# Block sums of an FFN written one tile ahead of their low parts, PSUM copies and weight sums in another order

## The chip, the cores and the metric

The kernel runs on one core of a Trainium2 chip. The metric is device microseconds of one execution; a time stands for the median of several runs. TensorE (PE) multiplies 128x128 blocks into PSUM, VectorE (DVE) and ScalarE (ACT) do the elementwise work, SyncE (SP) and GpSimd (POOL) issue the transfers.

## The reference

One decoder block on 1024 tokens of width 1024, all in float32. The change touches only the entry of its last part, the feed-forward network:

```python
h2 = rmsnorm(x, norm2_g[l]) * (1.0 + sc2) + sh2
fg, fu = jnp.split(h2 @ w_ffn_in[l], 2, axis=-1)
x = x + gt2 * ((jax.nn.silu(fg) * fu) @ w_ffn_out[l])
```

`h2` is 1024x1024, `w_ffn_in` 1024x5632 (2816 columns for `fg`, 2816 for `fu`). Ahead of it stand the attention branch, the convolution branch and the output projection, behind it the product with `w_ffn_out` and a last norm.

## The kernel before

Activations lie transposed: tile `x1[m]` (m = 0 to 7) holds 128 of the 1024 features for all tokens, the first half of the tokens in its columns up to 512 and the second half behind them. For a result near float32 each operand is kept as a high part, rounded to the type fp32r, and a low part (the operand less its high part); `mm3` issues three matmuls for one product of blocks: high by high, low by high, high by low. ScalarE writes the high part (`split_hi`, or an activation with a bias), VectorE subtracts to get the low part, so each split goes VectorE, ScalarE, VectorE.

The product `h2 @ w_ffn_in` is done in a form of seven block products instead of eight (class `Pair`, its table `PRODUCTS`). The activations are cut in four blocks A11, A12, A21, A22 (features by tokens), 256 columns of the weights in B11 to B22. Sums of blocks are formed: on the activation side S1, S2, S3, S4 (four tiles each, in place of `x1`'s columns), on the weight side T1, T2, T3, T4 (names `tt`, two halves of one tile `t` per pair). Product `p` of a pair is 12 matmuls of 512 columns into bank X, Z or Y (`fx`, `fz`, `fy`). Banks X and Z go on accumulating after a part of them has been copied out: `keep` copies a bank into a `kept` tile on ScalarE, `out` adds it and makes the hidden tile `g`. A product that accumulates into a bank waits until the copies out of it are done.

Pairs come in order 0 to 21. Even pairs belong to `fg`, odd ones to `fu`. The first two pairs are done together, since the activation sums are formed while they run: this is the code written out at the end of the function's FFN entry (from `both(6, 7)` on). There the order on each of TensorE, VectorE and ScalarE is the order of the code (`in_order(True, (T, V, A))`), and an engine works strictly down its list. It goes: products 0 and 5 (on A11 and A12), S1 and product 1, S2 and product 2, S4 and product 3, S3 and product 4, A22 and product 6. `staged(f, g)` runs two functions over the four tiles of a block: in the kernel before, `g(j-1)` (the low part of a tile) is written ahead of `f(j)` (scaling and sum of the next one). `evacuations(p)` calls `keep` or `out` for both pairs; the numbers of `both(...)` count weight blocks: 6 and 7 are T2, 8 and 9 B22, 10 and 11 T3, 12 and 13 T4 of the pairs 0 and 1, 14 and 15 B11 and T1 of pair 2, 16 its T2. From product 14 on (pair 2) the loop prepares up to two weight blocks ahead of each product, at most six ahead.

Of the kernel before, what the change touches and what calls it, by code (L numbers as in the profile page):

```python
# [30 lines left out]
HB = 512  # L31
# [62 lines left out]
def tile_hybrid_block(ctx: ExitStack, tc: tile.TileContext, xT, vecs, cvec, lamv, relb, bsel, bmask, jrev,  # L94
# [39 lines left out]
    def slot(name, dt=F32):  # L134
        return sp.tile([P, S], dt, tag="s4", name=name)

    def t2(name, dt=F32):
        return tp.tile([P, HB], dt, tag="t2", name=name)
# [13 lines left out]
    def split_hi(dst, src, scale=1.0):  # L152
        return A.activation(dst, src, AF.Copy, scale=scale)
# [11 lines left out]
    class Weights:  # L165
# [13 lines left out]
        def high(self):  # L179
            self.hi = wp.tile([P, D], F32R, tag="whi", name=f"wh_{self.name}")  # L180
            split_hi(self.hi[:, :self.n], self.raw[:, :self.n])

        def low(self):
            self.lo = wp.tile([P, D], F32R, tag="wlo", name=f"wl_{self.name}")
            V.tensor_tensor(out=self.lo[:, :self.n], in0=self.raw[:, :self.n], in1=self.hi.bitcast(F32)[:, :self.n],
                            op=ALU.subtract)
# [178 lines left out]
    with tc.tile_pool(name="psS", bufs=2, space=bass.MemoryType.PSUM) as psS, \  # L365
# [54 lines left out]
        with tc.tile_pool(name="st", bufs=2) as st:  # L420
# [61 lines left out]
            for k in range(KD):  # L482
# [3 lines left out]
                if k in KS:  # L486
                    j = KS.index(k)
# [408 lines left out]
    with tc.tile_pool(name="ps2", bufs=6, space=bass.MemoryType.PSUM) as ps2, ExitStack() as fxs:  # L896
# [69 lines left out]
        stages = dict(zip(CN, (cn.means, cn.center, squares, cn.scales, cn.finish)))  # L966
# [185 lines left out]
        class Pair:  # L1152
# [33 lines left out]
            def prepare(self, p):  # L1186
                self.low(self.high(p))

            def high(self, p):
                name = self.PRODUCTS[p][1]  # L1190
                src = self.source(name)
                w = self.w[name] = weight_block()
                split_hi(w[:, :HB], src)
                return w, src
# [70 lines left out]
        def weight_block():  # L1265
            n = nblock[0] % NWB
            nblock[0] += 1
            if n < NWB - 4:
                return fx[0].tile([P, D], F32R, tag="wb", name="wb", bufs=NWB - 4)
            return wp.tile([P, D], F32R, tag="whi" if n % 2 else "wlo", name="wbp")  # L1270
# [5 lines left out]
        def both(*ns):  # L1276

            parts = [(order[n][0], order[n][0].high(order[n][1])) for n in ns]
            for g, part in parts:
                g.low(part)  # L1280

        def staged(*stages):

            for i in range(KH + len(stages) - 1):
                for k, f in reversed(list(enumerate(stages))):
                    if 0 <= i - k < KH:
                        f(i - k)

        def new_block(name):
            acts[name] = [None] * KH  # L1290

        sums1 = {}

        def scale1(j):

            for m in (j, KH + j):
                norms[1].scale(m)
            acts["S1"][j] = slot(f"S1_{j}", F32R)
            t = sums1[j] = t2("s1")
            V.tensor_tensor(out=t, in0=x1[j][:, HB:], in1=x1[KH + j][:, HB:], op=ALU.add)  # L1300
            A.activation(acts["S1"][j][:, :HB], t, AF.Identity, bias=bsum[:, j:j + 1])
            for m in (j, KH + j):
                norms[1].shift(m)
# [14 lines left out]
        def sums(j):  # L1318

            a11, a21, a22 = x1[j][:, :HB], x1[j][:, HB:], x1[KH + j][:, HB:]  # L1320
            V.tensor_tensor(out=a21, in0=a11, in1=a21, op=ALU.subtract)
            V.tensor_tensor(out=a11, in0=a22, in1=a21, op=ALU.subtract)
            high("S2", j, a11)

        def sum4(j):
            a12 = x1[KH + j][:, :HB]
            V.tensor_tensor(out=a12, in0=a12, in1=x1[j][:, :HB], op=ALU.subtract)
            high("S4", j, a12)

        def blocks(name, get):  # L1330
            new_block(name)
            staged(lambda j: high(name, j, get(j)), lambda j: low(name, j, get(j)))
# [8 lines left out]
        two = pairs[:2]  # L1341
        V.tensor_tensor(out=bsum, in0=cols[:, 3 * KD:3 * KD + KH], in1=cols[:, 3 * KD + KH:4 * KD], op=ALU.add)

        def products(p):
            for k in range(KH):
                for g in two:
                    g.product(p, (k,))

        def evacuations(p):
            for g in two:  # L1350
                g.evacuate(p)

        both(6, 7)
        two[0].product(0)
        norms[1].stat()
        both(8, 9)
        two[1].product(0)
        new_block("S1")
        for g in two:
            g.product(5)  # L1360
        staged(scale1, low1)
        evacuations(0)
        products(1)
        evacuations(5)
        new_block("S2")
        staged(sums, lambda j: low("S2", j, x1[j][:, :HB]))
        evacuations(1)
        products(2)
        new_block("S4")
        staged(sum4, lambda j: low("S4", j, x1[KH + j][:, :HB]))  # L1370
        evacuations(2)
        products(3)
        both(10, 11)
        both(12, 13)
        pairs[2].load()
        pairs[3].load()
        blocks("S3", lambda j: x1[j][:, HB:])
        evacuations(3)
        for g in two:
            g.product(4)  # L1380
        blocks("A22", lambda j: x1[KH + j][:, HB:])
        both(14, 15)
        evacuations(4)
        for g in two:
            g.product(6)
        both(16)
        evacuations(6)
        nprep = 17

        late = {}  # L1390
# [40 lines left out]
        for gi, grp in enumerate(groups):  # L1431
# [17 lines left out]
            else:  # L1449
# [36 lines left out]
                for i, hs in enumerate(parts):  # L1486
# [3 lines left out]
                    for m in range(KD):  # L1490
# [4 lines left out]
                        t = x1[m][:, hs]  # L1495
# [83 lines left out]
```

## Time and profile before

| | |
|---|---|
| median of 3 runs | 1428.28 us (1426.91 to 1430.82) |
| the profiled execution | 1425.09 us, of which its span is 1423.3 us |
| TensorE busy | 1365.6 us (96% of the span), 6178 matmuls |
| VectorE busy | 982.9 us (69%) |
| ScalarE busy | 599.3 us (42%) |
| the first two FFN pairs | from 719 to 787 us of the span |

Busy time of TensorE counts pipelined matmuls, which overlap by some 0.16 us each, so 96% is not full speed. In the timeline a row is an instruction or a run of like ones on one engine with its start, its duration and, in brackets, how long the engine was idle before it and which engine's result ended that.

### The profile page before, as it was taken

The page shows a single profiled execution, that of the slowest core. Times are in us where ns is not written, and L with a number is a line of the kernel's source. Part 1 is how long each engine was busy: PE and PEld are TensorE (multiplying, and loading weights), DVE is VectorE, ACT ScalarE, POOL GpSimd, SP SyncE. Part 2 cuts the span into 40 slices and gives each one's busy share as a digit, 9 for nine tenths or more (in the row PEclk, how much of TensorE's full clock was granted, in tenths as well). Part 3 has the DMA queues.
Part 4 walks back from the last instruction along what each step waited for, and adds up shares of the span by engine and source line. Part 5 has one row for each costly group of instructions (what it writes and reads, how often), then busy time and mean ns, then how long its engine had stood idle before and what let it go on. Part 6 is the DMA issues. An engine that isn't in the chain of part 4 may idle for free.

```text
span 1423.3 us, 16124 instructions
## 1 busy us (share of the span) xinstructions
PE 1365.6 (96%) x6178; PEld 1114.0 (78%) x6178; DVE 982.9 (69%) x1588; ACT 599.3 (42%) x974; POOL 72.0 (5%) x84
## 2 busy tenths in 40 slices
PE   6799999999999999999977999999999999999996
PEld 4578888777788887888755888888888888888886
DVE  6947688899989897897868556666555555434345
ACT  4437676676611115632664433333333332202145
POOL 3400000000000000000100000000000000000004
PEclk8999999999999999999998999999999999999998
DMA  7511000100112123349501233332222335413203
GB/s 275 194 29 45 30 31 30 35 26 30 45 45 59 45 80 97 105 160 345 191 29 59 89 119 118 119 113 80 79 85 89 111 126 177 144 45 104 78 16 119
DMA packets 44271, 135.11 MB, mean 95 GB/s; under 512 B 4857, under 2 KB 7841, under 8 KB 44194
## 3 DMA queue, kind: packets, MB, share of 16 engines
q1 hardware_dynamic: 39458, 118.88, 25.1%
q0 software_dynamic: 4160, 14.68, 3.0%
q8 instruction: 48, 0.79, 0.2%
q10 hardware_dynamic: 576, 0.52, 0.1%
q14 instruction: 29, 0.24, 0.1%
HBM read 115.19 MB, written 18.88 MB: 94 GB/s over the span
## 4 chain that ended last, share of the span: by engine, by line
PE 79%; DVE 10%; ACT 6%; DMA 3%; issue 1%; POOL 1%; SPq 0%; DVEq 0%; ACTq 0%; POOLq 0%
PE fx L107 16%; PE fo L119 16%; PE proj L107 8%; PE fz L107 8%; PE gc L107 6%; PE ga L107 5%; PE fy L107 4%; PE oc L119 3%; PE oa L107 3%; PE wo L119 2%; PE sc L107 2%; DVE adac L119 2%; PE av L107 2%; DMA ada<-in_w_ada 1%; DMA wr_wo<-in_w_out 1%
## 5 line engine op out<-in xcount | busy, mean ns | idle before, releaser
L119 DVE SCALAR_TENSOR_TENSOR x1r<-fo,cols,x1r 128x512 f32<-128x512 f32 (+1 forms) x72 | 49.3, 689 | 119.8 <-PE fo L119 119.5
L119 PE MATMUL fo<-gl,wh_fo 128*128 128x512 f32 x288 | 112.2, 389 | 0.0
L119 PE MATMUL fo<-gh,wl_fo 128*128 128x512 f32 x288 | 112.1, 389 | 0.0
L119 PE MATMUL fo<-gh,wh_fo 128*128 128x512 f32 x288 | 111.9, 389 | 0.0
L107 DVE SCALAR_TENSOR_TENSOR cacc<-u,vec,cacc 128x1022 f32<-128x1022 f32 (+28 forms) x87 | 110.2, 1267 | 2.2
L107 PE MATMUL proj<-hhi,wh_in 128*128 128x512 f32 x239 | 98.3, 411 | 1.8 <-DVE kl L119 1.8
L107 PE MATMUL proj<-hhi,wl_in 128*128 128x512 f32 x240 | 94.0, 392 | 0.0
L107 PE MATMUL proj<-hlo,wh_in 128*128 128x512 f32 x240 | 93.7, 390 | 0.0
L107 PE MATMUL fz<-S,wb 128*128 128x512 f32 x312 | 76.5, 391 | 5.1 <-ACT S L107 4.3
L107 PE MATMUL fx<-S,wb 128*128 128x512 f32 x312 | 77.4, 398 | 3.6 <-ACT S L107 3.5
L107 PE MATMUL fx<-A,wb 128*128 128x512 f32 x335 | 79.2, 391 | 1.7 <-DVE g L107 1.7
L119 ACT ACTIVATE wh_fo<-wr_fo 128x768 fp32r<-128x768 f32 x24 | 20.3, 846 | 136.0 <-PE fo L119 130.5
L107 PEld LDWEIGHTS fx<-A,wb 128*128 128x128 f32 x335 | 62.8, 188 | 15.5 <-issue 2.5
L107 PEld LDWEIGHTS fx<-S,wb 128*128 128x128 f32 x312 | 60.0, 193 | 17.1 <-ACT S L107 4.0
L107 PEld LDWEIGHTS fz<-S,wb 128*128 128x128 f32 x312 | 58.2, 188 | 19.3 <-ACT S L107 5.6
L107 DVE TENSOR_TENSOR wb<-tt,wb 128x512 fp32r<-128x512 f32 x52 | 35.8, 692 | 45.4 <-ACT wb L107 45.1
L119 PEld LDWEIGHTS fo<-gl,wh_fo 128*128 128x128 f32 x288 | 54.1, 188 | 11.6 <-DVE gl L119 0.4
L119 PEld LDWEIGHTS fo<-gh,wh_fo 128*128 128x128 f32 x288 | 54.1, 188 | 11.3
L119 PEld LDWEIGHTS fo<-gh,wl_fo 128*128 128x128 f32 x288 | 54.1, 188 | 11.1
L107 PE MATMUL fx<-S,wbp 128*128 128x512 f32 x216 | 55.7, 408 | 5.3 <-ACT S L107 5.1
L107 ACT ACTIVATE wb<-tt 128x512 fp32r<-128x512 f32 x52 | 32.7, 629 | 61.7 <-DVE tt L107 61.5
L119 ACT ACTIVATE e<-sc,mn 128x512 f32<-128x512 f32 (+7 forms) x64 | 47.2, 740 | 26.9 <-DVE mn L119 25.9
(333 smaller groups left out, 3409.7 us busy)
## 6 DMA issues: line engine op xcount, KB each, us to landing
ada<-in_w_ada SPq DMA_DIRECT2D x32, 512.0 KB, 4.3
rawu<-in_w_fi SPq DMA_DIRECT2D x22, 512.0 KB, 3.5
rawg<-in_w_fi SPq DMA_DIRECT2D x22, 512.0 KB, 4.4
g_d<-g POOLq DMA_DIRECT2D x20, 512.0 KB, 4.2
gl<-g_d SPq DMA_DIRECT2D x20, 512.0 KB, 6.2
wr_fo<-in_w_fo SPq DMA_DIRECT2D x24, 384.0 KB, 3.1
adac<-in_w_ada SPq DMA_DIRECT2D x16, 512.0 KB, 4.3
wr_wo<-in_w_out SPq DMA_DIRECT2D x16, 512.0 KB, 5.2
```

The lines of the kernel that those rows point to most:

```text
L107: self.last = f(*args, **kw)
L119: self.last = self.chain(f, *args, **kw) if self.chain else f(*args, **kw)
```

## The change

In seven places the order of the instructions is changed; what is computed stays the same.

- `staged` no longer reverses its stages: `f(j)`, the scaling and sum of the next tile, is written ahead of `g(j-1)`, the low part of the tile before. All five blocks that use it are affected (S1, S2, S4, S3, A22).
- The S1 sums go into the free upper half of the pairs' `t` tiles instead of tiles of the pool `t2`.
- `both(8, 9)` moves ahead of the second norm's statistic.
- `evacuations(0)` moves ahead of S1, `evacuations(5)` behind S2.
- T3 and T4 of both pairs are computed one after the other, and `high` finds them there. The loads of pairs 2 and 3 are issued right behind them.
- `both(12, 13)` moves behind product 4, `both(14, 15)` behind product 6.
- `prepare(16)` moves behind `evacuations(6)`.

```diff
-                src = self.source(name)
+                src = self.b[name] if name in self.b else self.source(name)
...
-                for k, f in reversed(list(enumerate(stages))):
+                for k, f in enumerate(stages):
...
-            t = sums1[j] = t2("s1")
+            t = sums1[j] = two[j % 2].t[:, HB:]
...
-        both(6, 7)
+        both(6, 7, 8, 9)
         two[0].product(0)
         norms[1].stat()
-        both(8, 9)
         two[1].product(0)
+        evacuations(0)
         new_block("S1")
         for g in two:
             g.product(5)
         staged(scale1, low1)
-        evacuations(0)
         products(1)
-        evacuations(5)
         new_block("S2")
         staged(sums, lambda j: low("S2", j, x1[j][:, :HB]))
+        evacuations(5)
         evacuations(1)
         products(2)
         new_block("S4")
         staged(sum4, lambda j: low("S4", j, x1[KH + j][:, :HB]))
         evacuations(2)
         products(3)
-        both(10, 11)
-        both(12, 13)
+        for t in ("T3", "T4"):
+            for g in two:
+                g.source(t)
         pairs[2].load()
         pairs[3].load()
+        both(10, 11)
         blocks("S3", lambda j: x1[j][:, HB:])
         evacuations(3)
         for g in two:
             g.product(4)
+        both(12, 13)
         blocks("A22", lambda j: x1[KH + j][:, HB:])
-        both(14, 15)
         evacuations(4)
         for g in two:
             g.product(6)
-        both(16)
+        both(14, 15)
         evacuations(6)
+        prepare(16)
```

VectorE at S1, tiles 0 and 1 (`x_0_...` and `x_4_...` are `x1[0]` and `x1[4]`, `s_...` and now `tt` the sum, `S_0_...` the tile whose low part is written):

```order
 L107 SCALAR_TENSOR_TENSOR x_0_4949<-x_0_4949,cols,rstd 128x512
 L107 SCALAR_TENSOR_TENSOR x_4_5112<-x_4_5112,cols,rstd 128x512
-L107 TENSOR_TENSOR s_5749<-x_0_4949,x_4_5112 128x512
-L107 SCALAR_TENSOR_TENSOR S_0_5748<-s_5749,small,S_0_5748 128x512
+L107 TENSOR_TENSOR tt<-x_0_4949,x_4_5112 128x512
 L107 SCALAR_TENSOR_TENSOR x_1_4992<-x_1_4992,cols,rstd 128x512
 L107 SCALAR_TENSOR_TENSOR x_5_5150<-x_5_5150,cols,rstd 128x512
-L107 TENSOR_TENSOR s_5758<-x_1_4992,x_5_5150 128x512
-L107 SCALAR_TENSOR_TENSOR S_1_5757<-s_5758,small,S_1_5757 128x512
+L107 TENSOR_TENSOR tt<-x_1_4992,x_5_5150 128x512
+L107 SCALAR_TENSOR_TENSOR S_0_5752<-tt,small,S_0_5752 128x512
```

The low part of tile 0 now stands behind the sum of tile 1; the others follow in the same way.

VectorE from the last tile of S2 to the first of S4 (`g_...`, `kepta`: the three instructions of `evacuations(5)`, which stood ahead of S2 before):

```order
+L107 TENSOR_TENSOR S_2_5819<-x_2_5030,S_2_5819 128x512
+L107 TENSOR_TENSOR S_3_5824<-x_3_5068,S_3_5824 128x512
+L107 TENSOR_TENSOR g_5828<-fy,kepta 128x512
+L107 TENSOR_TENSOR kepta<-fy,kepta 128x512
+L107 TENSOR_TENSOR g_5828<-kepta,g_5828 128x512
 L107 TENSOR_TENSOR x_4_5112<-x_4_5112,x_0_4949 128x512
-L107 TENSOR_TENSOR S_0_5866<-x_4_5112,S_0_5866 128x512
 L107 TENSOR_TENSOR x_5_5150<-x_5_5150,x_1_4992 128x512
+L107 TENSOR_TENSOR S_0_5862<-x_4_5112,S_0_5862 128x512
```

S4 begins behind the copies out of bank Y, and its low parts too are one tile late.

ScalarE from the second norm's statistic to S1 (`rstd` is the norm's factor by Ln and Exp, `wbp` the high parts of weight blocks 8 and 9, `kepta` the copies of `evacuations(0)`):

```order
+L107 ACTIVATE wbp<-rawg 128x512
+L119 ACTIVATE sq<-x_7_5282 128x512
+L107 ACTIVATE wbp<-rawu 128x512
 L107 ACT_TABLE_LOAD
-L119 ACTIVATE sq<-x_7_5282 128x512
-L107 ACTIVATE rstd<-st_5694,small 128x512
+L107 ACTIVATE rstd<-st_5700,small 128x512
 L107 ACT_TABLE_LOAD
 L107 ACTIVATE rstd<-rstd 128x512
-L107 ACTIVATE wbp<-rawg 128x512
-L107 ACTIVATE wbp<-rawu 128x512
-L107 ACTIVATE S_0_5748<-s_5749,small 128x512
+L107 ACTIVATE kepta<-fx 128x512 x2
+L107 ACTIVATE S_0_5752<-tt,small 128x512
```

The two high parts stand ahead of Ln and Exp, and the copies out of bank X between Exp and the first high part of S1.

## Rows read from the trace of the kernel before

**Rows 1.** Busy time by stretch: us, then each engine's busy time, TensorE's granted clock, DMA
```profile
719.00:787.00 68.00, 51.42 (x177) 34.89 (x176) 47.68 (x74) 35.38 (x56) 1.08 (x2) 0.90 0.11 43
787.00:1400.00 613.00, 613.00 (x2759) 509.33 (x2758) 326.68 (x483) 204.59 (x322) 16.69 (x24) 1.00 0.29 99
```

**Rows 2.** Timeline of TensorE: start, us, what, and the idle time before it
```profile
731.78 1.56 PE L107 MATMUL fz<-S,wb 128*128 128x512 f32 x6
...
748.90 7.69 PE L107 MATMUL fx<-S,wbp 128*128 128x512 f32 x18 [4.63 <-ACT S L107]
...
770.72 8.28 PE L107 MATMUL fx<-S,wb 128*128 128x512 f32 x24 [3.54 <-ACT S L107]
780.66 8.42 PE L107 MATMUL fx<-A,wb 128*128 128x512 f32 x36 [1.66 <-DVE g L107]
```

**Rows 3.** Timeline of VectorE from the second norm to the last wait
```profile
726.97 0.69 DVE L107 TENSOR_TENSOR wbp<-rawg,wbp 128x512 fp32r<-128x512 f32 x1 [5.15 <-ACT wbp L107]
...
728.18 1.41 DVE L107 SCALAR_TENSOR_TENSOR x<-x,cols,rstd 128x512 f32<-128x512 f32 x2
729.62 0.69 DVE L107 TENSOR_TENSOR s<-x,x 128x512 f32<-128x512 f32 x1
731.11 0.75 DVE L107 SCALAR_TENSOR_TENSOR S<-s,small,S 128x512 fp32r<-128x512 f32 x1 [0.80 <-ACT S L107]
...
742.03 0.75 DVE L107 SCALAR_TENSOR_TENSOR S<-s,small,S 128x512 fp32r<-128x512 f32 x1 [0.79 <-ACT S L107]
743.74 0.69 DVE L107 TENSOR_TENSOR g<-fy,kepta 128x512 f32<-128x512 f32 x1 [0.96 <-ACT kepta L107]
...
746.16 0.69 DVE L107 TENSOR_TENSOR g<-kepta,g 128x512 f32<-128x512 f32 x1 [1.14 <-ACT g L107]
746.77 0.68 DVE L107 TENSOR_TENSOR x<-x 128x512 f32<-128x512 f32 x1
747.49 0.69 DVE L107 TENSOR_TENSOR x<-x,x 128x512 f32<-128x512 f32 x1
748.88 0.69 DVE L107 TENSOR_TENSOR S<-x,S 128x512 fp32r<-128x512 f32 x1 [0.69 <-ACT S L107]
...
757.63 0.69 DVE L107 TENSOR_TENSOR x<-x,x 128x512 f32<-128x512 f32 x1
...
765.60 0.69 DVE L107 TENSOR_TENSOR tt<-rawg 128x512 f32<-128x512 f32 x1
...
770.79 2.49 DVE L107 TENSOR_TENSOR S<-x,S 128x512 fp32r<-128x512 f32 x4
...
779.83 0.68 DVE L107 TENSOR_TENSOR g<-fx,keptc 128x512 f32<-128x512 f32 x1
```

**Rows 4.** Timeline of ScalarE in the same stretch
```profile
723.78 0.69 ACT L107 ACTIVATE rstd<-st,small 128x512 f32<-128x512 f32 x1 [1.22 <-PE st L107]
...
725.78 0.63 ACT L107 ACTIVATE rstd<-rstd 128x512 f32<-128x512 f32 x1
...
743.13 1.06 ACT L107 ACTIVATE kepta<-fx 128x512 f32<-128x512 f32 x2
744.21 1.28 ACT L107 ACT_TABLE_LOAD   x1
...
770.05 2.18 ACT L107 ACTIVATE S<-x 128x512 fp32r<-128x512 f32 x4
```

**Rows 5.** Busy time by stretch where the granted clock was low, columns as above
```profile
748.00:757.00 9.00, 7.69 (x18) 4.82 (x18) 6.13 (x10) 2.53 (x5) 0.00 (x0) 0.62 0.00 0
...
767.00:777.00 10.00, 6.45 (x17) 4.67 (x17) 9.65 (x16) 6.57 (x12) 0.00 (x0) 0.66 0.56 210
...
1414.00:1416.00 2.00, 1.15 (x2) 0.43 (x2) 0.00 (x0) 1.26 (x3) 1.19 (x2) 0.52 0.50 175
```

**Rows 6.** Timeline of TensorE at the kernel's end
```profile
1412.44 2.72 PE L119 MATMUL stf<-sq,ones 128*128 128x256 f32 x6 [2.49 <-DVE sq L119]
```

**Rows 7.** DMA issues of the page: out<-in, KB each, us to landing
```profile
rawg<-in_w_fi SPq DMA_DIRECT2D x22, 512.0 KB, 4.4
```

## The prediction

> **What bounds the kernel now.** I read busy time by stretch first. From 787 to 1400 us TensorE is busy all the time at the full clock; from 719 to 787 it is busy 51.4 of 68.0 us and its clock averages 0.90 [rows 1]. The change touches only this stretch; what it gains there moves everything behind it, which runs at TensorE's pace and has no wait to take the gain back. So the question is when product 6 of the first two pairs can start, 780.66 us before.
>
> Then the timeline of TensorE: every long wait in the stretch is for S, A or g, results of ScalarE or VectorE [rows 2]. VectorE and ScalarE are themselves busy 47.7 and 35.4 us only [rows 1], and the timeline of VectorE shows why: it waits 0.69 to 0.80 us for ScalarE's high part before each low part, tile after tile [rows 3], while ScalarE waits for VectorE's next sum. The two take turns. The chain from the norm to product 6 is VectorE's list with these waits in it; I work the new list through in the same way.
>
> **Durations.** On VectorE a tensor_tensor starts 0.60 us after the one ahead where nothing holds it (four in 2.49 us, 0.69 each), and 0.72 after one that it depends on (746.77 to 747.49). A scalar_tensor_tensor frees VectorE after 0.67 (two in 1.41). From the end of a sum to the start of its low part, through ScalarE, 0.70 us pass (747.49 + 0.69 to 748.88), 0.80 in S1 (730.31 to 731.11) [rows 3]. I take these for the new order too. The bounds are 0.60 and 0.69 per instruction beside a busy ScalarE; the nearest row is the one where both engines run four S instructions at once, 770.05 and 770.79, and neither is slowed [rows 3, 4]: I take 0.60.
>
> **The change step by step**, from the first scaling (728.18) on:
>
> 1. *Blocks 8 and 9 ahead of the norm.* Exp ends at 725.78 + 0.63 = 726.41 [rows 4]. Scaling now starts 1.77 us later, since two high parts and two low parts stand between [rows 3]. They move to where VectorE idles 5.15 us and ScalarE 1.22 us before Ln [rows 3, 4]; two copies of 0.53 fit in 1.22. Gain 1.8; if that cover were gone, Ln would come up to 1.1 later and 0.7 would be left.
>
> 2. *S1.* Before, 14.5 us from the first scaling to the point where VectorE is free behind the last low part (742.03 + 0.67). After: scalings and sum of a tile take 1.44 + 0.60 = 2.04, a low part 0.67. The fourth sum starts at 4 x 2.04 - 0.60 + 2 x 0.67 = 8.90, ends at 9.59; the last low part waits 0.80, starts at 10.39 and frees VectorE at 11.06. Gain 3.45. The copies of bank X (1.06 us for two) [rows 4] now stand ahead of the first high part on ScalarE. They need 725.78 + 0.53 + 1.06 = 727.4, and the first sum ends at 726.4 + 1.44 + 0.69 = 728.6: hidden, 1.2 us to spare.
>
> 3. *Evacuation 5 leaves the place between S1 and S2.* Before, from 742.70 to 746.77: waits for the two copies, the table load of 1.28 us and ScalarE's g [rows 3, 4]. Gain 4.07. It costs 2.0 behind S2: the first add 0.69, ScalarE's g 0.70, the product 0.60; the second add lies within. The table load runs while VectorE does the last low parts.
>
> 4. *S2.* Before 746.77 to 757.63, 10.86. After: 1.32 a tile for the two subtractions, 0.61 a low part. The second subtraction of tile 3 starts at 3 x 1.32 + 2 x 0.61 + 0.72 = 5.90; its low part at 5.90 + 0.69 + 0.70 = 7.29; free at 7.90. Gain 2.96.
>
> 5. *S4.* Before 757.63 to 765.60, 7.97. After: the first low part at 1.39, then 0.60 each: fourth subtraction at 3.20, its low part at 4.59, free at 5.19. Gain 2.78.
>
> 6. *T3 to evacuation 4.* Before 765.60 to 779.83, 14.2 us with 22 instructions ahead of evacuation 4. After, 19 (T1 and the low parts of blocks 14 and 15 go behind it): 19 x 0.60 plus some 0.4 us of waits = 11.8. Gain 2.4.
>
> Sum: 1.8 + 3.45 + 4.07 - 2.0 + 2.96 + 2.78 + 2.4 = 15.5 us. Evacuation 4 would run at 779.83 - 15.5 = 764.4, product 6 start 0.83 behind it, as before, at 765.2.
>
> TensorE keeps up: at the full clock a tile of two pairs is 6 matmuls of 0.23 us (36 in 8.42) [rows 2], 1.4 us, less than VectorE's 2.7, 1.9 and 1.2 to 1.4 a tile. The loads of pairs 2 and 3 go out behind T4, some 9 us ahead of evacuation 4; a load lands in 4.4 us [rows 7]. What stands behind product 6 (blocks 14 to 16) has its 24 matmuls, 5.5 us, as cover for 14 and 15.
>
> **What takes some of it back: the clock.** Product 4 can't end before its last low part is there: nine instructions behind T3's first, 5.4 + 0.7, then some 15 matmuls, so 9.5 us after it; product 6 starts at 12.6. That leaves TensorE idle for about 3.1 us, against 1.66 there before [rows 2]. In this trace idle times of 4.63 and 3.54 [rows 2] and of 2.49 us [rows 6] are followed by the lower level [rows 5], 1.2 GHz, 1.66 isn't. By the low averages, (1 - 0.62) x 2 x 9 and (1 - 0.66) x 2 x 10, it lasted 6.8 us each time [rows 5]. Before, VectorE was the bound there and it cost little. Behind product 6 TensorE is the bound, and half of the low time is lost: 3.4, or less where it begins in the idle time. I take 3.0 and think it more likely than not. Gain 12.5. From the median shown that is 1428.3 - 12.5 = 1415.8; the profiled execution, 1425.1 with 1423.3 of span, would be 1412.6. It lies 3.2 under the median, and I take the difference as the same for both kernels.
>
> The page "VectorE: DVE Perf Modes" of the Trainium skill (section "The DRAIN you can't avoid") has a rule against the change: the next instruction starts only when the pipe of the one ahead is empty. By it the filled waits would hold full-length instructions. The rows show 0.60 start to start where one takes 0.69, so the trace doesn't agree for independent ones, and the sum goes by the rows; by the rule it would be the rival with 0.69 below.
>
> **The rivals.**
>
> - *The clock doesn't fall ahead of product 6*, or falls earlier, at S4, where VectorE is still the bound. For it: 3.1 us lies between 1.66 and 3.54, though 2.49 speaks against. 1428.3 - 15.5 = 1412.8.
> - *VectorE's instructions take 0.69 start to start* once the waits are filled and ScalarE works beside it. Some 45 instructions of the new chain stand at 0.60 or 0.67, 45 x 0.085 = 3.8 us: 1428.3 - 12.5 + 3.8 = 1419.6. Against: the four in 2.49 us.
> - *The clock is low through the whole stretch*, so that the change does its part on VectorE and TensorE becomes the bound. Ten products from 731.8 at 12 x 0.43 (18 matmuls in 7.69) [rows 2] are 51 us; with 0.8 for evacuation 4 product 6 ends at 783.8, against 780.66 + 5.5 = 786.1: 1426.0, no change. Against: a busy TensorE got its clock back after 6.8 us [rows 5], and it is busier now.
> - *Slower: the lead of the weight blocks is lost at pair 2.* Block 16 is prepared behind evacuation 6, which waits for product 6's end, 5.5 us after its start plus 0.4. Evacuation, subtraction, high part and low part then take 0.6 + 0.7 + 0.7 + 0.7, so block 16 is ready some 9 us after product 6's start. It is needed four products of 2.75 us after it (product 6 twice, then products 0 and 1 of pair 2), at 11 us: 2 us to spare. If it is late, each following preparation stands on VectorE behind an evacuation that waits for TensorE, and each product waits some 2.1 us. Over the 14 products of pairs 2 and 3 that is 29 us, and the time 1428.3 - 15.5 + 29 = 1442. It decides from the second product of pair 2 on. Against: up to two blocks are prepared per product, 1.2 us each on VectorE, so the lead comes back.
>
> **How the numbers follow.** Clock falls at product 6, gain 12.5: chance 0.52, own range 1413 to 1418.5. No fall there: 0.30. Instructions at 0.69: 0.07. Low clock throughout: 0.08. Lead lost: 0.03. The time predicted is that of the first, 1415.8 us. The range reaches to the no-fall case with the scatter of the three runs (some 2 us) below it and to a little over the 0.69 case above: 1410 to 1421; outside lie the last two and the tails, together about 0.17. A measurement of this kernel can tell about 0.3%, 4.3 us, from no change. Faster by more than that are the first three, 0.89; the same 0.08; slower 0.03.
>
> **What would show it.** In the changed profile: scaling starts within 0.1 us of Exp's end; low parts of S1 about 2.7 us apart, of S2 1.9, of S4 1.2, with waits on ScalarE only at the last of each; evacuation 5 behind S2 with a wait under 0.3 us; product 6 starting at about 765 with 3 us of idle time ahead; the clock low for some 6.8 us from there in the first case, not in the second. From pair 2 on TensorE without a wait. I am wrong if product 6 starts later than 769, or if waits for weight blocks appear behind it.

## The result, and the profile after

The changed kernel takes 1412.1 us (median of 4 runs, 1409.8 to 1413.2) against 1427.7 us before (4 runs, 1426.9 to 1430.8): a ratio of 0.988, 95% interval 0.986 to 0.991. That is 15.6 us less where 12.5 were forecast. The profiled execution takes 1409.76 us with 1408.0 of span, 15.3 less than that of before.

Busy time by stretch, columns as in [rows 1], the changed kernel:

```profile
719.00:773.00 54.00, 45.30 (x184) 33.56 (x183) 46.10 (x73) 35.07 (x56) 1.61 (x3) 1.00 0.16 57
773.00:1386.00 613.00, 613.00 (x2762) 508.86 (x2761) 327.84 (x484) 204.90 (x323) 17.48 (x24) 1.00 0.30 99
```

VectorE and ScalarE are busy nearly as long as in [rows 1] (46.1 and 35.1 us), but in 54 us instead of 68, and TensorE is without work for 8.7 us instead of 16.6. In the 613 us behind it TensorE is busy throughout, as before. VectorE's timeline of the changed kernel, against [rows 3]:

```profile
725.78 1.41 DVE L107 SCALAR_TENSOR_TENSOR x<-x,cols,rstd 128x512 f32<-128x512 f32 x2 [3.36 <-ACT rstd L107]
727.23 0.69 DVE L107 TENSOR_TENSOR tt<-x,x 128x512 f32<-128x512 f32 x1
727.84 1.41 DVE L107 SCALAR_TENSOR_TENSOR x<-x,cols,rstd 128x512 f32<-128x512 f32 x2
729.28 0.69 DVE L107 TENSOR_TENSOR tt<-x,x 128x512 f32<-128x512 f32 x1
729.89 0.74 DVE L107 SCALAR_TENSOR_TENSOR S<-tt,small,S 128x512 fp32r<-128x512 f32 x1
...
736.86 0.68 DVE L107 TENSOR_TENSOR x<-x 128x512 f32<-128x512 f32 x1
...
744.76 0.68 DVE L107 TENSOR_TENSOR g<-fy,kepta 128x512 f32<-128x512 f32 x1
...
746.75 1.29 DVE L107 TENSOR_TENSOR x<-x,x 128x512 f32<-128x512 f32 x2
...
751.94 0.68 DVE L107 TENSOR_TENSOR tt<-rawg 128x512 f32<-128x512 f32 x1
...
763.81 0.68 DVE L107 TENSOR_TENSOR g<-fx,keptc 128x512 f32<-128x512 f32 x1
```

The next tile's sum (729.28) stands ahead of S's low part (729.89), and the brackets of 0.69 to 0.80 us are gone: between 725.78 and 763.81 VectorE still waits for ScalarE at the last tile of a block, at S4's first low part and behind a g, at most 0.16 us each time. The stages read off as the distances of these rows. TensorE in the same execution, against [rows 2]:

```profile
718.48 0.39 PE L104 MATMUL fx<-A,wb 128*128 128x512 f32 x1
...
764.64 8.44 PE L107 MATMUL fx<-A,wb 128*128 128x512 f32 x36 [2.84 <-DVE g L107]
```

The first row is the first matmul of product 0 of the first pair. From there to product 6 the changed kernel takes 46.16 us. Before, it took 61.79 (718.87 to 780.66), so 15.63 less. From here on places are given from that first matmul, since it starts between 717.4 and 721.6 us in the ten profiled executions of kernels whose code is the same up to there: the kernel's front, all that runs ahead of it, scatters by more than most parts of the change are worth. A place itself is good to some 0.3 us: the changed kernel's second profile, below, has product 6 at 46.44.

### The profile page after: what moved, and what is told of

Read it like the earlier page. It is cut to its first block, busy times and chain, and to the rows that moved or that the text cites. A ratio compares the mean times of both kernels' runs of the same rounds, so it can differ in the third digit from the quotient of the medians.

```text
span 1408.0 us, 16120 instructions
## 1 busy us (share of the span) xinstructions
PE 1363.6 (97%) x6178; PEld 1115.1 (79%) x6178; DVE 981.6 (70%) x1588; ACT 598.8 (43%) x974; POOL 72.0 (5%) x84
## 4 chain that ended last, share of the span: by engine, by line
PE 81%; DVE 10%; ACT 5%; DMA 2%; issue 1%; POOL 1%; SPq 0%; DVEq 0%; ACTq 0%; POOLq 0%
PE fx L107 16%; PE fo L119 16%; PE proj L107 9%; PE fz L107 8%; PE gc L107 6%; PE ga L107 5%; PE fy L107 4%; PE oc L119 3%; PE oa L107 3%; PE wo L119 3%; PE sc L107 2%; DVE adac L119 2%; PE av L107 2%; PE wps L107 1%; PE vacc L119 1%
## 5 line engine op out<-in xcount | busy, mean ns | idle before, releaser
L107 PEld LDWEIGHTS proj<-hhi,wh_in 128*128 128x128 f32 x239 | 45.4, 190 | 11.3 <-issue 3.6
```

Of the source, the lines that this page charges most:

```text
L107: self.last = f(*args, **kw)
```

## The experiments

**The changed kernel once more.** No edit. 

> The changed kernel once more, unaltered. Its four runs were 1409.8, 1411.2, 1413.0 and 1413.2 us with a mean granted clock of 0.991, 0.990, 0.989 and 0.989, and the one that was profiled (1409.8) shows no fall of the clock ahead of product 6, where a fall was forecast. Theory A: in some runs the clock falls in the idle time ahead of product 6 (2.84 us in the profile), in others it doesn't; then the time of a run goes with its mean clock, some 3.3 us for 0.0024 (6.8 us at half of 1408), and new runs fall into the same span of times. Rival: the spread comes from elsewhere (the loads at the kernel's start), and time and mean clock don't go together.

Measured: 1413.0 us (5 runs, 1411.2 to 1416.1), ratio to before 0.992 (0.991 to 0.993). In this series the kernel before takes 1425.3 us (9 runs), so the gain is 12.3 us here, where it was 15.6 in the first series. Time and mean clock don't go together (1411.2 at 0.990, 1413.0 at 0.991, 1416.1 at 0.989), and the places above say where much of the spread is made, ahead of the change. So theory A is not borne out as the cause of the spread, though the mean clock is a weak test, since it also counts low stretches at the kernel's start and end. But the profiled execution shows the fall that was forecast. TensorE's timeline:

```profile
717.85 0.39 PE L104 MATMUL fx<-A,wb 128*128 128x512 f32 x1
...
764.29 9.93 PE L107 MATMUL fx<-A,wb 128*128 128x512 f32 x36 [2.81 <-DVE g L107]
```

The stretches at the start of that product, columns as in [rows 1]:

```profile
764.00:766.00 2.00, 1.71 (x4) 1.45 (x5) 1.90 (x4) 1.15 (x2) 0.16 (x1) 0.53 0.00 0
766.00:768.00 2.00, 2.00 (x7) 1.52 (x7) 1.44 (x3) 0.63 (x1) 0.38 (x1) 0.62 0.55 225
```

After 2.81 us of idle time the clock is low for (0.47 + 0.38) x 2 x 2 = 3.4 us, and 36 matmuls take 9.93 us instead of 8.44: 1.5 us. In the first profile, after 2.84 us, it stays up.

**Matmuls in the idle time.** Nine matmuls with an unused result ahead of product 6:

```diff
+FILL = 9
...
         evacuations(4)
+        fill = bankG("fill")
+        for _ in range(FILL):
+            T.matmul(fill, acts["A22"][0][:, :P], acts["A22"][0][:, :HB], start=True, stop=True)
         for g in two:
             g.product(6)
```

> Nine matmuls of 512 columns whose result nobody reads are put on TensorE between product 4 and product 6 of the first two pairs: 2.0 us of work in the 2.84 us that it is idle there. They hold nothing up: product 6 starts at the same place within 0.2 us. Theory A (a fall of the clock there in some runs): no run falls any more, all at about 1409.8, the spread under 2 us, the median some 2 us below the changed kernel's. Rival (spread from elsewhere): median about 1412 and the same spread.

Measured: 1409.8 us (4 runs), ratio 0.989 (0.988 to 0.991), on the chip of the run above, 3.2 us under its median. Three runs lie at 1409.1 to 1410.3. The fourth, at 1413.1, is the profiled one, and its product 0 starts late on TensorE's timeline:

```profile
721.57 0.39 PE L105 MATMUL fx<-A,wb 128*128 128x512 f32 x1
...
767.73 8.45 PE L108 MATMUL fx<-A,wb 128*128 128x512 f32 x36 [0.71 <-DVE g L108]
```

Product 6 is at 46.16 us, where it was, at full speed. From the first matmul to the end of the span this profile takes 689.7 us, the changed kernel's two take 689.5 without the fall and 691.6 with it. The sign is as theory A has it; the intervals of the times just touch, so by the times the size of the difference is not shown.

**A longer idle time.** Blocks 14 and 15 ahead of evacuation 4 again:

```diff
+        both(14, 15)
         evacuations(4)
         for g in two:
             g.product(6)
-        both(14, 15)
```

> Blocks 14 and 15 go back ahead of evacuation 4 (as in the kernel before), nothing else: T1 and two low parts with one wait for ScalarE, about 2.0 us, so product 6 starts at about 766.6 and TensorE is idle for 4.8 us ahead of it. Theory A: the clock falls there in every run, product 6 and what follows pay about 3 us: 1409.8 + 2.0 + 3 = 1414.8. Rival (no fall, or it costs nothing): 1411.8 to 1414.0, the changed kernel's median plus 2.

Measured: 1414.7 us (5 runs), ratio 0.992 (0.991 to 0.994). TensorE's timeline:

```profile
719.67 0.39 PE L104 MATMUL fx<-A,wb 128*128 128x512 f32 x1
...
767.83 9.76 PE L107 MATMUL fx<-A,wb 128*128 128x512 f32 x36 [4.83 <-DVE g L107]
```

Product 6 comes 48.16 us after product 0, 2.0 later, and the clock fell; the fall cost 1.3 us of 9.76, not 3. The median agrees with theory A, but by the scatter of the front it would not tell 1.3 from 3.

**The skew undone, and the skew alone.** The line of `staged` in the changed kernel back, and the new line in the kernel before:

```diff
-                for k, f in enumerate(stages):
+                for k, f in reversed(list(enumerate(stages))):
```

> The changed kernel with the low part of a tile written ahead of the next tile's sum again (the one line of the stages' order), all else as changed. Theory (VectorE and ScalarE take turns): S1, S2 and S4 lose what the skew gave, 3.45 + 2.96 + 2.78 = 9.2 us by the prediction's terms; product 6 starts at about 773.8, time about 1421. Rival (the placement of the evacuations is what counts, and the waits would be hidden without the skew): under 3 us lost, 1415 or less.

> The kernel before with the skew alone. Theory: the terms of S1, S2 and S4, 9.2 us, are gained by themselves: product 6 at about 771.5 instead of 780.7, time about 1418.5. Rival: the terms overlap with the other parts (the turn of bank X and Y evacuations between S1 and S2 still stands), so alone it gives 5 us or less.

Measured: 1419.7 us, ratio 0.996 (0.995 to 0.997), without the skew; 1417.2 us, ratio 0.995 (0.993 to 0.996), with nothing but it. TensorE's timeline without the skew:

```profile
717.41 0.39 PE L104 MATMUL fx<-A,wb 128*128 128x512 f32 x1
...
772.60 8.45 PE L107 MATMUL fx<-A,wb 128*128 128x512 f32 x36 [1.21 <-DVE g L107]
```

And with the skew alone:

```profile
719.34 0.39 PE L104 MATMUL fx<-A,wb 128*128 128x512 f32 x1
...
771.81 10.03 PE L107 MATMUL fx<-A,wb 128*128 128x512 f32 x36 [3.62 <-DVE g L107]
```

Undone, product 6 comes at 55.19 us, 9.0 later than in the changed kernel; alone, at 52.47, 9.3 earlier than in the kernel before. The terms were 9.2 and they add up with the other parts. Both rivals fall. The new place of the S1 sums was not tested by itself; the skew alone brought its 9.3 us without it.

**Evacuations 0 and 5 back.**

```diff
         two[1].product(0)
-        evacuations(0)
...
         staged(scale1, low1)
+        evacuations(0)
         products(1)
+        evacuations(5)
...
-        evacuations(5)
         evacuations(1)
```

> The changed kernel with evacuations 0 and 5 back at their places around product 1 (0 behind S1, 5 ahead of S2). Theory: the net of the terms 4.07 - 2.0, so 2.1 us lost: product 6 at about 766.7; TensorE gets an idle time of about 4 us ahead of S2 again and its clock falls there, which costs nothing at product 6, since VectorE's list is the bound. Rival (the fall of the clock costs as well): 4 us or more.

Measured: 1412.1 us (4 runs), ratio 0.992 (0.989 to 0.994). TensorE's timeline:

```profile
718.29 0.39 PE L104 MATMUL fx<-A,wb 128*128 128x512 f32 x1
...
742.87 0.80 PE L107 MATMUL fx<-S,wbp 128*128 128x512 f32 x1 [4.14 <-ACT S L107]
...
766.54 8.44 PE L107 MATMUL fx<-A,wb 128*128 128x512 f32 x36 [2.84 <-DVE g L107]
```

Product 6 at 48.25, 2.1 later. TensorE idles 4.14 us ahead of S2 and its clock is low there (0.66 on average from 740 to 750 us), and that costs nothing more at product 6: what is lost where VectorE sets the pace is free. The time can't show it, being 0.9 us under that of the changed kernel's second series, on another chip; the places in the profile can.

**Blocks 8 and 9 behind the statistic.**

```diff
-        both(6, 7, 8, 9)
+        both(6, 7)
         two[0].product(0)
         norms[1].stat()
+        both(8, 9)
```

> The changed kernel with blocks 8 and 9 behind the norm's statistic again. Theory: scaling starts 1.8 us later and so does product 6 (766.4); time 1.8 us up. Rival: the two high and two low parts are hidden elsewhere, 0.5 us or less.

Measured: 1412.9 us (4 runs), ratio 0.992 (0.990 to 0.993). TensorE's timeline:

```profile
718.11 0.39 PE L104 MATMUL fx<-A,wb 128*128 128x512 f32 x1
...
765.99 10.05 PE L107 MATMUL fx<-A,wb 128*128 128x512 f32 x36 [2.80 <-DVE g L107]
```

Product 6 at 47.88, 1.7 later as the term had it (1.8); here too the clock fell, after 2.80 us.

**The order from T3 on undone.** T3 and T4 apart, blocks 12 to 16 at their old places:

```diff
-        for t in ("T3", "T4"):
-            for g in two:
-                g.source(t)
+        both(10, 11)
+        both(12, 13)
         pairs[2].load()
         pairs[3].load()
-        both(10, 11)
...
-        both(12, 13)
         blocks("A22", lambda j: x1[KH + j][:, HB:])
+        both(14, 15)
         evacuations(4)
...
-        both(14, 15)
+        both(16)
         evacuations(6)
-        prepare(16)
```

> The changed kernel with the order of the kernel before from T3 on (blocks 10 to 13, then S3, A22, blocks 14 and 15, evacuation 4, product 6, block 16). Theory: VectorE's 22 instead of 19 instructions ahead of evacuation 4 cost 2.4 us, product 6 starts 48.5 us after product 0 instead of 46.2; behind it 19.14 us to product 5 of pair 2. With the smaller idle time ahead of product 4 or 6 the clock may or may not fall. Net 1.8 us slower than the changed kernel. Rival (the weight sums written together are worth nothing, only their distance counts): product 6 within 0.5 us of 46.2.

Measured: 1413.2 us (4 runs), ratio 0.991 (0.989 to 0.992); the changed kernel wasn't run on that chip. TensorE's timeline:

```profile
719.83 0.39 PE L104 MATMUL fx<-A,wb 128*128 128x512 f32 x1
...
768.35 11.33 PE L107 MATMUL fx<-A,wb 128*128 128x512 f32 x36 [3.59 <-DVE g L107]
...
790.40 2.88 PE L107 MATMUL fy<-A,wbp 128*128 128x512 f32 x12
```

Product 6 at 48.52, 2.4 later. The clock fell and 36 matmuls took 11.33 us, 2.9 more: here it was low for 6.8 us (averages of 0.92, 0.50, 0.50, 0.50 and 0.88 in the five stretches of 2 us from 766 to 776).

**Block 16 ahead of evacuation 6.**

```diff
-        evacuations(6)
         prepare(16)
+        evacuations(6)
```

> The changed kernel with block 16 prepared ahead of evacuation 6 again, as in the kernel before, nothing else. Theory (small loss of the weight blocks' lead): VectorE waits 2.6 us for product 6 in evacuation 6, and ScalarE's copies out of banks X and Z of pair 2 stand behind late high parts; with block 16 ahead of it the 0.6 us come back, product 6 to product 5 of pair 2 takes 19.14 us as before instead of 19.76. Rival (they come from blocks 14 and 15 behind product 6): 19.5 or more.

Measured: 1411.5 us (4 runs), ratio 0.990 (0.988 to 0.991). TensorE's timeline, product 5 of pair 2 in the kernel before:

```profile
799.80 2.88 PE L107 MATMUL fy<-A,wbp 128*128 128x512 f32 x12
```

In the changed kernel:

```profile
784.40 2.88 PE L107 MATMUL fy<-A,wbp 128*128 128x512 f32 x12
```

And here, with product 6 above it:

```profile
763.93 10.03 PE L107 MATMUL fx<-A,wb 128*128 128x512 f32 x36 [2.83 <-DVE g L107]
...
784.68 2.88 PE L107 MATMUL fy<-A,wbp 128*128 128x512 f32 x12
```

From product 6 on it is 19.14 us before, 19.76 after and 20.75 here; the clock fell here, 10.03 against 8.44 for 36 matmuls, and less these 1.59 it is 19.16. So 0.6 us come back, by a difference of two rows. The run above, which has block 16 ahead of evacuation 6 too, agrees: 22.05 us from product 6 to product 5 of pair 2 (768.35 to 790.40), and 19.16 less the 2.89 of its fall. The waits of the changed kernel's weight loads on TensorE from 771 to 788 us (us in total, times, longest; the two longest of four) name what it was:

```profile
PEld fz L107 <- ACT keptc L107: 0.4, 1, 0.4
PEld fx L107 <- ACT keptb L107: 0.4, 1, 0.4
```

The copies out of pair 2's banks stood on ScalarE behind high parts that came late.

**A shorter idle time.** Half of evacuation 4 ahead of A22:

```diff
         both(12, 13)
+        two[0].evacuate(4)
         blocks("A22", lambda j: x1[KH + j][:, HB:])
-        evacuations(4)
+        two[1].evacuate(4)
```

> The copy out of pair 0's bank (half of evacuation 4) is written ahead of the low parts of A22, and product 6 of pair 0 can start as soon as product 4 of pair 1 ends. Worked from the changed kernel's timeline: the first half of evacuation 4 starts at 761.2 instead of 763.8, product 6 at some 762.0 instead of 764.6, ends some 2.3 us earlier; idle ahead of it under 0.3 us, then one wait of under 0.8 us inside. Theory A: that shift and no fall in any run, about 1407.5 with a small spread, 4.5 us under the changed kernel's median. Rival: the shift alone, 1409.8 median with the same spread as the changed kernel. If VectorE's list is not the bound there, no shift.

Measured: 1410.4 us (4 runs, 1410.0 to 1411.2), ratio 0.989 (0.988 to 0.991). TensorE's timeline:

```profile
719.35 0.39 PE L104 MATMUL fx<-A,wb 128*128 128x512 f32 x1
...
764.02 0.50 PE L107 MATMUL fx<-A,wb 128*128 128x512 f32 x1 [1.34 <-ACT A L107]
764.75 8.33 PE L107 MATMUL fx<-A,wb 128*128 128x512 f32 x35 [0.22 <-DVE A L107]
```

A miss in part: product 6 starts at 44.67, 1.5 earlier instead of 2.6, and TensorE waits for a high part of A22. On ScalarE evacuation 4's g now stands ahead of it, and that waits for VectorE. The 36 matmuls end 0.9 us earlier (53.73 against 54.60).

**That repaired, with block 16 ahead of evacuation 6.** The edit is against the changed kernel:

```diff
-        blocks("A22", lambda j: x1[KH + j][:, HB:])
-        evacuations(4)
+        new_block("A22")
+        for j in range(2):
+            high("A22", j, x1[KH + j][:, HB:])
+        two[0].evacuate(4)
+        for j in range(KH):
+            low("A22", j, x1[KH + j][:, HB:])
+            if j + 2 < KH:
+                high("A22", j + 2, x1[KH + j + 2][:, HB:])
+        two[1].evacuate(4)
...
+        prepare(16)
         evacuations(6)
-        prepare(16)
```

> The changed kernel with the first half of evacuation 4 ahead of the low parts of A22, two high parts of A22 written ahead of it on ScalarE (in the run without them product 6 waited 1.34 us for such a high part, which stood behind evacuation 4's g on ScalarE), and block 16 prepared ahead of evacuation 6. Theory: product 6 starts 43.6 us after product 0 (46.16 in the changed kernel), less than 0.6 us idle in and ahead of it, and from product 6 to product 5 of pair 2 as in the kernel before (19.1 us instead of 19.8): 2.4 + 0.6 us and no fall of the clock there, so some 3 us under the changed kernel's undisturbed runs and 4 to 5 under its median, a ratio of about 0.988. Rival (VectorE's list is the bound, a wait moves from product 6's first half to its second): no more than the 0.9 us that the run without the two high parts gained by the profile.

Measured: 1407.4 us (4 runs, 1407.0 to 1408.0), ratio 0.987 (0.986 to 0.989): the fastest of all, some 5 us under the changed kernel's medians of 1412.1 and 1413.0, the second of them on another chip. TensorE's timeline:

```profile
718.42 0.39 PE L104 MATMUL fx<-A,wb 128*128 128x512 f32 x1
...
761.98 8.84 PE L107 MATMUL fx<-A,wb 128*128 128x512 f32 x36 [0.24 <-DVE g L107]
781.72 2.88 PE L107 MATMUL fy<-A,wbp 128*128 128x512 f32 x12
```

Product 6 at 43.56, as worked out; product 5 of pair 2 at 63.30 against 65.92 in the changed kernel, 2.6 earlier where 3.0 were expected (0.4 stay inside product 6). From the first matmul to the end of the span it takes 686.8 us, 2.7 less than the changed kernel's profile without a fall and 4.8 less than the one with it. That both profiles of a filled idle time show no fall is in line with theory A, but two profiles don't prove that it never falls there.

## Why the prediction was right, point by point

**The bound** was read rightly: VectorE's list set the start of product 6 and TensorE nearly everything behind it. The 15.3 us of the two profiled executions are 0.39 from the front, 15.63 up to product 6, less 0.62 just behind it and 0.1 further on. That the first series' medians differ by just the 15.6 us of the sum is in part luck: the front of a run alone scatters by 4 us, and in the second series the medians differ by 12.3.

**The terms**, forecast and then measured in the changed kernel's rows against [rows 3, 4]:

| step | forecast gain | measured |
|---|---|---|
| 1, blocks 8 and 9 | 1.8 | 2.0 (728.18 - 718.87 before, 725.78 - 718.48 after); 1.7 when undone |
| 2, S1 | 3.45 | 3.44 (14.52 to 11.08) |
| 3, evacuation 5 away from S1 | 4.07 | 4.07, since S2 now starts at once behind S1; cost behind S2 2.0, measured 1.99 |
| 4, S2 | 2.96 | 2.96 (10.86 to 7.90) |
| 5, S4 | 2.78 | 2.78 (7.97 to 5.19) |
| 6, T3 to evacuation 4 | 2.4 | 2.36 (14.23 to 11.87); 2.4 when undone |
| sum | 15.5 | 15.6 |

They came out so near because each instruction's duration stood in a row and the new list could be walked one instruction after the other, ScalarE's trip included. The value of 0.60 us start to start held with both engines at work: steps 2 to 6 of the changed kernel agree within 0.05 us and step 1 within 0.2, so the rival with 0.69 falls. The rule that stood beside it from the Trainium skill (page "VectorE: DVE Perf Modes", section "The DRAIN you can't avoid") is half of what that section says: it goes on that a next instruction that is not held, so need not wait until the earlier ones have finished, starts earlier. These rows agree with that: they start 0.60 us apart and take 0.69 each.

**The clock** is the term that was mis-sized. The idle time ahead of product 6 was forecast at 3.1 us and is 2.8. A fall was called more likely than not at 3.0 us. Five profiles have that idle time at 2.80 to 2.84 us (the changed kernel twice, evacuations back, blocks 8 and 9 back, block 16 ahead): three show the fall, two don't, and it cost 1.5 to 1.6 us, with 3.4 us at the low level. The forecast took the length of the idle time for what decides, and both low stretches of the kernel before, 6.8 us each [rows 5], for the rule. That half of the low time is lost where TensorE is the bound was about right (1.5 to 1.6 of 3.4). So the expected cost was nearer 1 than 3, and the first rival, 1412.8, was nearer the time than the forecast, 1415.8. The one profile among the four runs of the result has no fall, as in that rival; for the other three it is not known.

**Behind product 6** the forecast saw no wait. There are 0.6 us: block 16 and what follows are prepared late, as the rival of the lost lead said, but what is late for TensorE are the copies out of the banks on ScalarE, not the weights, and the lead is back within pair 3. From product 5 of pair 2 to that of pair 3 it is 19.10 us against 19.04 before, and 19.04 for every later pair in both.

The rival of a low clock throughout did not show: no low average stands in the stretch in the first profile of the changed kernel.

The scatter of the front is made in two places for the most part. Near 319 us the clock falls in some profiles and not in others, and a wait for weights of the output projection, near 678 us, comes out longer or shorter. Up to 316 us the ten profiles come apart by 0.6 us only; the fall costs 0.8 to 2.0 us, and the stretch from the output projection's first matmul to product 0 takes 89.4 to 91.4 us. The kernel before, then the changed kernel, at the fall (columns as in [rows 1]):

```profile
320.00:330.00 10.00, 9.36 (x41) 7.43 (x41) 9.94 (x19) 4.21 (x7) 0.00 (x0) 1.00 0.17 52
320.00:330.00 10.00, 10.00 (x39) 8.15 (x38) 9.97 (x19) 4.00 (x7) 0.00 (x0) 0.83 0.16 52
```

The longest wait for the weights, with the order from T3 undone:

```profile
678.83 0.50 PE L119 MATMUL wo<-yh,wh_wo 128*128 128x512 f32 x1 [1.30 <-ACT wh_wo L119]
```

What stays open: which chance lets the clock fall after 2.8 us in one execution and not in another, why those weights come late in some, and why the kernel before is 2.4 us faster in the second series than in the first.

## What to carry to other kernels

Where two engines take turns on a chain of tiles, write the next tile's first step ahead of this tile's last, and move out of the chain what only needs to come sometime; the gain can be worked out beforehand by walking the list of the engine that sets the pace. Measure parts of a change by places within one execution (here from the first matmul of the stage), when the time of a run scatters by more than a part is worth. A strict order has a price at its far end: what is put off comes back in front of something on another engine, here a g ahead of a high part, and copies out of banks behind late weight blocks.

## What the runs showed of the hardware

After the same idle time of TensorE, 2.80 to 2.84 us, the granted clock was at its lower level, 1.2 GHz, in three profiles and full in two. At product 6 the low stretches lasted 3.4 us five times (three of those profiles, after 4.83 us idle, and after 3.62 with the skew alone) and 6.8 us once (after 3.59 us, the order from T3 undone); the kernel before has two of 6.8 us further ahead [rows 5]. So their length did not follow the idle time. Nor does a fall need a long wait. Without the skew the clock fell at 765.2 us behind waits of 0.94 and 1.32 us:

```profile
762.42 0.50 PE L107 MATMUL fx<-S,wb 128*128 128x512 f32 x1 [0.94 <-ACT S L107]
764.25 7.13 PE L107 MATMUL fx<-S,wb 128*128 128x512 f32 x23 [1.32 <-DVE S L107]
```

```profile
764.00:766.00 2.00, 1.75 (x6) 1.44 (x7) 2.00 (x5) 0.63 (x1) 0.00 (x0) 0.80 0.93 332
766.00:768.00 2.00, 2.00 (x6) 1.52 (x6) 1.84 (x4) 1.31 (x3) 0.00 (x0) 0.50 0.87 334
```

And near 319 us it fell in five of all thirteen profiles behind short waits, none over 1.0 us, which the other eight have too. A fall at product 6, where TensorE was the bound, cost 1.3 to 1.6 or 2.9 us, one near 319 us 0.8 to 2.0 us, and one ahead of product 6, where VectorE was the bound, nothing.
